# An eight-core decoder layer in fp32: norm factors applied after the matmul instead of before it, and the per-layer-embedding stage placed inside the next tile's first FFN

## The chip, the cores and the metric

The kernel runs on all eight cores of one Trainium2 chip, two dies of four cores. Each core works on one of the eight prompt sequences and on 16 of the 128 sampled tokens, with no exchange between cores. The time is device microseconds (us) of the slowest core. Each execution is called fast or slow: slow when one die runs over 1% longer than the other at a lower granted TensorE clock, or when the run is over 1.5% above the fastest of its kernel.

Different chips were used for different batches of runs, and the kernel before took between 1880 and 1950 us on them. So I compare ratios to the kernel before from the same batch, and, inside the traces, a lost time that leaves the chip's own slower clock out (explained below). In the views of the profile PE is TensorE and PEld its weight loads, DVE is VectorE, ACT ScalarE, POOL GpSimd. PSUM is the memory into which matmuls write, here in eight banks; reading a result out of it is called evacuation. A word is four bytes on each of the 128 partitions.

## The reference, cut to what matters

```python
D_MODEL, BATCH, SEQ, DEC_BATCH, PLE_DIM, D_FF = 1024, 8, 2048, 128, 256, 2816

def rms_norm(x, g):
    return x * rsqrt(mean(x * x, -1) + 1e-6) * g

def swiglu(x, w_gate, w_up, w_down):
    return (silu(x @ w_gate) * (x @ w_up)) @ w_down

def decoder_layer(x, p, s0, conv0, ng, ...):
    h = x + 0.5 * rms_norm(swiglu(rms_norm(x, ng[0]), f1_gate, f1_up, f1_down), ng[1])
    mix, s_new, conv_new = token_mixer(rms_norm(h, ng[2]), ...)   # linear attention in chunks + short conv
    h = h + rms_norm(mix, ng[3])
    h = h + 0.5 * rms_norm(swiglu(rms_norm(h, ng[4]), f2_gate, f2_up, f2_down), ng[5])
    gate = sigmoid(rms_norm(h, ng[6]) @ w_ple_gate)
    h = h + rms_norm((p @ w_ple_proj) * gate, ng[7])
    return h, s_new, conv_new
# ... called once for the prompt and once for the sampled tokens; all fp32
```

There are four stages (FFN1, mixer, FFN2, per-layer embedding), and each has a norm before it and a norm after it. The factor of a norm, rsqrt(mean(x*x)), is one number for a token. So (x*g) @ W times the factor is the same as the normalised x @ W: the factor may be applied after the matmul.

## The kernel before

A core cuts its 2048 tokens into eight tiles of 256 (the third has 272: the sampled tokens ride along). Two tiles, "slot 0" and "slot 1", go through the layer side by side and form a pair; they share every weight piece while it is in the chip. The features lie on the partitions, so the mean over features is a matmul with a matrix of 1/1024, and a factor for each token comes out on all partitions.

The order of the instructions of each engine is fixed when the program is built: generators yield operations, and a list scheduler with its own cost figures emits the one that can start first. On TensorE slot 0 goes first until it is LEAD words of weights ahead. Dependencies become semaphore waits.

```python
RING_W = 19456      # words per partition of the weight ring
LEAD = 8192         # slot 0's lead, in words of weights: 64 matmuls

# scheduler's own cost of a DMA:
self.dma_free = max(self.dma_free, start + 1.0) + op.nbytes / 320e3
self.fin[tok] = self.dma_free + 1.2

# pieces of weights in the order of their use; FFN columns are 2048 words (1 MB), then 1408 for the down projection
def w_issue():                                   # the ring: strictly first in, first out
    while wst["next"] < len(pieces):
        p = pieces[wst["next"]]
        lo = wst["head"]
        if lo + p["words"] > RING_W: lo = 0
        hi = lo + p["words"]
        live = wst["live"]
        while live and not live[0]["users"]: live.pop(0)     # a piece leaves when BOTH tiles have used it
        if any(q["at"] < hi and lo < q["at"] + q["words"] for q in live): return
        # ...
        P.emit_op(dma("pool", ...))

def h_squares(x): ...            # squares of h on ScalarE, sums on VectorE
def stats(x, scale=1.0):
    bk, = yield get_banks(1)
    yield mm(bk.v(0, x.n), [(csr.v(C_OD, C_OD + 128, r=True), x.accr())])      # mean by matmul
    yield act(x.lnt(), bk.v(0, x.n), AF.Ln, scale=scale, bias=eps)
    put_banks(bk)
    yield act(x.rs(), x.lnt(), AF.Exp, scale=-0.5)
def normalize(x, g):
    for c in range(8):
        yield stt(x.ch(x.xn, c, r=True), x.ch(x.h, c), ngl.v(g*8+c, ...), x.rs(), ALU.mult, ALU.mult)
def pre_norm(x, g):
    yield from h_squares(x); yield from stats(x); yield from normalize(x, g)
def post_norm(x):
    yield from stats(x)
    for q in range(4):                           # two 128-row chunks at a time
        yield tt(f2r, f2, rsb, ALU.mult)         # stage's result times its factor
        yield tt(h2, h2, f2, ALU.add)            # into the residual h

def slot(s):
    for t in range(s, NT, 2):
        x = T(t)
        yield lambda: True if t in loaded else None
        yield from pre_norm(x, 0)
        yield from ffn(x, 0, 1)                  # ends with post_norm
        yield from pre_norm(x, 2)
        yield from mixer(x)                      # ends with post_norm
        load_p(t)
        yield from pre_norm(x, 4)
        yield from ffn(x, 1, 5)
        yield from pre_norm(x, 6)
        yield from ple(x)
```

## Time and profile before

| | before |
|---|---|
| median of 3 runs (lowest to highest; the highest is a slow one) | 1880.64 us (1880.24 to 2009.39) |
| profiled fast run: span | 1891.0 us (core 4) |
| matmuls on each core | 11,554 |
| TensorE / VectorE / ScalarE busy | 79% / 42% / 36% |

The page of the profiled run begins with the span and the busy time of each engine (us, share, number of instructions):

```profile
span 1891.0 us, 33733 instructions; the slowest of 8 cores (1873.6 to 1891.0 us)
...
PE 1498.2 (79%) x11554; PEld 1464.5 (77%) x11554; DVE 787.8 (42%) x1730; ACT 684.0 (36%) x1533; POOL 222.6 (12%) x425
```

The list of what TensorE waited for (engine, written tile, source line <- who released it: total us, times, longest). L265 is the helper that emits nearly every matmul, L311 and L318 are VectorE helpers:

```profile
PE ps_pair L265 <- DVE sb_acc L311: 210.8, 33, 34.3
PE ps_pair L265 <- DVE sb_xn L318: 118.3, 23, 6.6
PE ps_pair L265 <- DVE sb_big L311: 23.4, 13, 5.3
```

The first line is the wait for the last addition of a sum of squares, the second the wait for normalised activations: 329 us together, of which 34.3 us is the start of the program and about 295 us are norms between stages. Nothing in this list is a DMA: the before never waits for weights.

One seam of this kind in the timeline of TensorE (start, length, operation, number of instructions, in brackets the idle time before it and what ended it): FFN2 to embedding stage to the next pair's FFN1.

```profile
1371.80 4.02 PE L265 MATMUL ps_pair<-sb_big,sb_ring 128*128 128x256 f32 x34
1377.80 0.35 PE L265 MATMUL ps_pair<-sb_acc,sb_csr 128*128 128x256 f32 x1 [1.99 <-DVE sb_acc L311]
1386.65 0.55 PE L265 MATMUL ps_pair<-sb_acc,sb_csr 128*128 128x256 f32 x1 [8.50 <-DVE sb_acc L311]
1391.79 2.05 PE L265 MATMUL ps_pair<-sb_xn,sb_ring 128*128 128x256 f32 x8 [4.58 <-DVE sb_xn L318]
```

The statistics matmul at 1377.80 belongs to the norm after FFN2, the one at 1386.65 to the norm before the embedding stage, and only at 1391.79 do the stage's own matmuls begin: 1.99 + 8.50 + 4.58 us of idle TensorE. Some 50 us later, before the next FFN1, it comes again.

**How I count lost time.** At full clock, matmuls with 256 columns start 118 ns apart. I took the start of every matmul from the trace. Where the next start comes more than 0.4 us later, the excess over 118 ns is a *pause*; where it comes sooner but the clock record says half speed, the excess is *half clock*. At a granted clock of 0.81 the spacing is 134 ns; I count that apart, because it depends on the chip. The matmuls are put to stages by the order of the program. All such numbers here are means over the eight cores. Before: 372 us pauses + 74 us half clock = 446 us lost (and 4 us at 0.81).

### The profile page before, as it was taken

The numbers are of one execution on the slowest core, as the hardware profiler recorded it, in microseconds if no ns is written. First come the engines' busy times: TensorE is split into PE (matmuls) and PEld (weight loads), VectorE is DVE, ScalarE is ACT, GpSimd is POOL, SyncE is SP. The second block draws the span as 40 slices with busy tenths as digits, with TensorE's granted clock in tenths as the row PEclk, the third lists the DMA queues.
The fourth block names the chain that finished last, engine by engine and source line by source line (L and its number), as shares of the span: only waits on it lengthen the run. The fifth ranks groups of instructions, "written<-read, shape, count | busy, mean of one in ns | idle before, by whom it ended". The sixth has DMA issues, their size and how long they took to land.

```text
span 1891.0 us, 33733 instructions; the slowest of 8 cores (1873.6 to 1891.0 us)
## 1 busy us (share of the span) xinstructions
PE 1499.8 (79%) x11554; PEld 1465.7 (78%) x11554; DVE 787.9 (42%) x1730; ACT 684.1 (36%) x1533; POOL 222.6 (12%) x425
## 2 busy tenths in 40 slices
PE   1797977996699686879658987869964996977964
PEld 1797877996599685779658987769964996967964
DVE  1223663115621576521454227642166216652145
ACT  1223464124522443422353234642244224552234
POOL 1011010110011110011100110101200120101100
PEclk9899897886799896789878998979977998988987
DMA  9499373984689662569855994739944995746951
GB/s 279 132 312 293 94 221 115 288 236 149 202 256 276 192 196 90 184 194 290 230 146 166 323 271 130 217 103 314 274 143 156 282 287 177 212 145 206 288 153 48
DMA packets 71334, 391.09 MB, mean 207 GB/s; under 512 B 8432, under 2 KB 9088, under 8 KB 38912
## 3 DMA queue, kind: packets, MB, share of 16 engines
q0 software_dynamic: 60512, 369.36, 65.3%
q1 hardware_dynamic: 10656, 19.58, 3.5%
q8 instruction: 97, 1.59, 0.3%
q14 instruction: 69, 0.57, 0.1%
HBM read 378.16 MB, written 10.75 MB: 206 GB/s over the span
## 4 chain that ended last, share of the span: by engine, by line
PE 71%; DVE 14%; issue 7%; ACT 5%; DMA 1%; DVEq 0%; SPq 0%; ACTq 0%
PE ps_pair L265 70%; DVE sb_xn L318 4%; ACT sb_scl L306 4%; DVE sb_h L311 2%; DVE sb_xn L311 2%; DVE sb_scl L311 2%; DMA sb_bg<-bg 1%; DVE sb_om L318 1%; PE ps_pair L276 1%; ACT L306 1%; DVE sb_big L311 1%; DVE sb_acc L311 1%; DVE sb_ring L311 0%; ACT sb_xn L306 0%; DVEq L218 0%
## 5 line engine op out<-in xcount | busy, mean ns | idle before, releaser
L265 PE MATMUL ps_pair<-sb_xn,sb_ring 128*128 128x256 f32 (+1 forms) x7424 | 974.2, 292 | 106.1 <-DVE sb_xn L318 98.4
L265 PEld LDWEIGHTS ps_pair<-sb_xn,sb_ring 128*128 128x128 f32 x7424 | 955.3, 201 | 114.0 <-issue 113.5
L311 DVE TENSOR_TENSOR sb_big<-ps_pair,sb_tmp 128x256 fp32r<-128x256 f32 (+1 forms) x384 | 163.3, 426 | 574.6 <-PE ps_pair L265 514.2
L306 ACT ACTIVATE sb_tmp<-ps_pair 128x256 f32<-128x256 f32 (+1 forms) x480 | 182.4, 384 | 532.8 <-PE ps_pair L265 528.0
L265 PE MATMUL ps_pair<-sb_big,sb_ring 128*128 128x256 f32 (+1 forms) x2816 | 347.0, 284 | 0.0
L265 PEld LDWEIGHTS ps_pair<-sb_big,sb_ring 128*128 128x128 f32 x2816 | 342.6, 192 | 0.0
L311 DVE TENSOR_TENSOR sb_scl<-sb_scl 128x256 f32<-128x256 f32 (+3 forms) x288 | 147.7, 515 | 326.2 <-ACT sb_scl L306 317.2
L265 PE MATMUL ps_pair<-sb_acc,sb_csr 128*128 128x256 f32 (+1 forms) x64 | 26.3, 411 | 209.5 <-DVE sb_acc L311 209.5
L265 PEld LDWEIGHTS ps_pair<-sb_acc,sb_csr 128*128 128x128 f32 x64 | 14.7, 230 | 216.9 <-issue 216.4
L306 ACT ACT_TABLE_LOAD x93 | 119.3, 1283 | 129.0 <-PE ps_pair L265 123.8
L306 ACT ACTIVATE sb_scl<-ps_pair 128x256 f32<-128x256 f32 (+1 forms) x192 | 73.9, 385 | 246.2 <-PE ps_pair L265 228.6
L318 DVE SCALAR_TENSOR_TENSOR sb_xn<-sb_h,sb_ngl,sb_scl 128x256 fp32r<-128x256 f32 (+1 forms) x256 | 104.7, 482 | 28.0 <-ACT sb_scl L306 27.5
L306 ACT ACTIVATE sb_scl<-sb_h 128x512 f32<-128x512 f32 (+1 forms) x128 | 76.4, 626 | 101.5 <-DVE sb_scl L311 96.2
L346 POOL DMA_DIRECT2D sb_ring<-f2a x88 | 46.5, 528 | 471.8 <-PE ps_pair L265 435.9
L346 POOL DMA_DIRECT2D sb_ring<-f1a x88 | 46.5, 533 | 467.5 <-PE ps_pair L265 467.5
L265 PE MATMUL ps_pair<-sb_om,sb_ring 128*128 128x256 f32 (+1 forms) x512 | 68.5, 295 | 6.6 <-DVE sb_om L311 6.6
L265 PEld LDWEIGHTS ps_pair<-sb_om,sb_ring 128*128 128x128 f32 x512 | 66.6, 201 | 8.1 <-issue 8.0
L311 DVE TENSOR_TENSOR sb_xn<-sb_xn,sb_scl 128x512 fp32r<-128x512 f32 (+1 forms) x96 | 66.3, 691 | 10.2 <-ACT sb_scl L306 9.0
L311 DVE TENSOR_TENSOR sb_h<-sb_h,sb_xn 128x512 f32<-128x512 f32 (+1 forms) x96 | 66.2, 692 | 4.5
L306 ACT ACTIVATE sb_xn<-ps_pair,sb_nglh 128x256 fp32r<-128x256 f32 (+1 forms) x128 | 60.3, 471 | 0.0
L306 ACT ACTIVATE sb_scl<-ps_pair,sb_cst 128x256 f32<-128x256 f32 (+2 forms) x80 | 41.2, 515 | 41.3 <-PE ps_pair L265 40.6
L346 POOL DMA_DIRECT2D sb_ring<-f2b x64 | 33.8, 530 | 145.9 <-PE ps_pair L265 145.7
(84 smaller groups left out, 824.9 us busy)
## 6 DMA issues: line engine op xcount, KB each, us to landing
sb_ring<-f1a POOLq DMA_DIRECT2D x88, 1024.0 KB, 11.7
sb_ring<-f2a POOLq DMA_DIRECT2D x88, 1024.0 KB, 10.3
sb_ring<-f1b POOLq DMA_DIRECT2D x64, 704.0 KB, 7.3
sb_ring<-f2b POOLq DMA_DIRECT2D x64, 704.0 KB, 7.1
sb_ring<-wca POOLq DMA_DIRECT2D x16, 1024.0 KB, 9.4
sb_ring<-wo POOLq DMA_DIRECT2D x16, 1024.0 KB, 10.9
sb_ring<-wpg POOLq DMA_DIRECT2D x16, 1024.0 KB, 7.3
sb_ring<-wv POOLq DMA_DIRECT2D x8, 1024.0 KB, 7.0
```

The lines of the kernel that those rows point to most:

```text
L265: ins = e.matmul(out.ap, a.ap, b.ap, start=(first and i == 0), stop=(last and i == n_ - 1), skip_group_check=skip)
L276: ins = e.matmul(o.ap, a.ap, b.ap, start=s, stop=t)
L306: return Op("act", lambda e: e.activation(out=out.ap, in_=in_.ap, func=func, **kw), rd, [out], 0.24 + 0.000833 * width(out), TSET.get(func))
L311: return Op(eng, lambda e: e.tensor_tensor(out=out.ap, in0=a.ap, in1=b.ap, op=op), [a, b], [out], 0.19 + width(out) / 960.0)
L318: return Op("dve", lambda e: e.scalar_tensor_tensor(out=out.ap, in0=a.ap, scalar=sc, in1=b.ap, op0=op0, op1=op1), rd, [out], 0.19 + width( ...
L346: return Op(eng, lambda e: e.dma_start(out=out, in_=in_), reads, writes, 0.55 if eng == "pool" else 0.1, None, name, nbytes, is_output)
```

## The change

The intent is to take the norms off TensorE's path in three ways.

1. *Deferral.* At a boundary the residual is only multiplied by its weight g, and the first matmuls of a stage take that raw product. The factor is made meanwhile and applied when the results are read out of PSUM (mixer gates, three FFN2 columns, embedding gate); for the other matmuls a `renorm` multiplies the raw copy beside the work.
2. *Move.* The embedding stage is spawned beside the next tile of its slot: its matmuls and weights are mixed into the first columns of the next pair's FFN1. That tile's own first norm (`prep`) is made ahead, during FFN2.
3. *Order.* Boundary operations go first on VectorE and ScalarE, Ln and Exp stay together, slot 0 leads by 80 matmuls instead of 64. A fourth residual buffer takes space, so the ring shrinks.

```diff
-RING_W = 19456
+RING_W = 16896
+NRAW = 3
+PLE_AT = (3, 5, 7, 9)
-LEAD = 8192
+LEAD = 10240
# ... cut: priorities (first, hold, free) of operations and their use in the scheduler
-        hb = [P.sbuf(f"h{i}", 128, 8 * TW) for i in range(3)]
+        hb = [P.sbuf(f"h{i}", 128, 8 * max(W_T[i::4])) for i in range(4)]
# ... weights of the embedding stage go between FFN1 columns of the next pair
+            def ple_w(pr, i):
+                piece((pr, "pg", i), wpg_d[...], 2048, tl)
+                piece((pr, "pp", i), wpp_d[...], 512, tl)
                 for j in range(NJ):
                     piece((pr, "a", f, j), fA_d[f][...], 2048, tl)
+                    if f == 0 and pr and j in PLE_AT:
+                        ple_w(pr - 1, PLE_AT.index(j))
# ... the boundary
-        def pre_norm(x, g):      # squares, statistics, eight multiplications
-        def post_norm(x):        # statistics, four times (multiply, add)
+        def boundary(x, g, buf):
+            yield from stats(x, [x.accr(0), x.accr(1)], x.rs(0))
+            x.pre = yield ("spawn", next_stats(x))            # next factor, beside the work
+            for q in range(4):
+                yield tt(x.pair3(f2r), x.pair3(f2), x.rs2(0), ALU.mult).first()
+                yield tt(x.ch(x.h, 2*q, 2), x.ch(x.h, 2*q, 2), f2, ALU.add).first()
+                hs.append((yield ("spawn", scaled(x, q, g, buf))))   # h * g, no factor, on ScalarE
+            yield join(hs)
# ... an FFN column on raw input: the factor at evacuation
+            if raw:
+                yield join([x.pre])
+                yield tt(t.v(0, x.n), bg_.v(0, x.n), x.rs(1), ALU.mult)
+                yield act(t.v(0, x.n), t.v(0, x.n), AF.Silu)
+                yield tt(t.v(0, x.n), t.v(0, x.n), x.rs(1), ALU.mult)
# ... FFN1 may overwrite the embedding stage's products from its column 14 on
+                if j == NJ - 8 and x.last:
+                    yield join([x.last])
# ... cut: sampled tile's values on GpSimd, merged additions of squares
         def slot(s):
+            tiles[s].prep = yield ("spawn", prep(tiles[s]))
             for t in range(s, NT, 2):
-                yield from pre_norm(x, 0)
                 yield from ffn(x, 0, 1)
-                yield from pre_norm(x, 2)
                 yield from mixer(x)
                 load_p(t)
-                yield from pre_norm(x, 4)
                 yield from ffn(x, 1, 5)
-                yield from pre_norm(x, 6)
-                yield from ple(x)
+                last = yield ("spawn", ple(x))
+                if t + 2 < NT:
+                    tiles[t + 2].last = last
```

## The prediction

> **What bounds the kernel now.** TensorE. The page shows it busy for 1500 of 1891 us, VectorE 42%, ScalarE 36%, DMA 207 GB/s. By the starts of core 0's matmuls, 10,765 of 11,554 run at full clock, 118 ns apart; 788 at half clock, 213 ns apart; 386 us are 95 pauses over 0.6 us. Without pauses and half clock the matmuls need about 1367 us. The list of waits names the pauses: TensorE waited 211 us in 33 waits for the last addition of a sum of squares and 118 us in 23 for the normalised activations; all others are below 25 us, none for weights. So 329 us are norms between stages; half clock costs about 74 us more (788 x 95 ns).
>
> One pair of tiles takes 447 us (1266 to 1713), of which 2872 matmuls need 339. Its pauses in the timeline: FFN1 to mixer 15 us, mixer and its end about 19, mixer to FFN2 14, FFN2 to embedding stage 16, embedding stage to next FFN1 20 + 6.
>
> **What the change does.**
> 1. The next matmul no longer waits for squares, sum, Ln, Exp and eight 0.48 us multiplications (14 us from the statistics matmul at 1377.8 to the first product at 1391.8). There remain last evacuation, one statistics matmul, Ln and Exp (0.9 us), four times two 0.69 us VectorE operations, one ScalarE scaling: 9 to 10 us. The lead of one tile over the other grows from 64 to 80 matmuls (9.4 us), which about fills that. Mixer gates and three FFN2 columns run on raw input while the second statistic is made.
> 2. The embedding stage moves inside the next FFN1; both its boundaries vanish for three of four pairs. The next tile's first norm is made ahead. About 42 us per pair.
> 3. Table loads (93 x 1.28 us; the Trainium skill, "ScalarE: Activation LUTs", What ACT_TABLE_LOAD costs, gives the same 1283 ns) leave the chain: Ln's table is fetched early, Ln and Exp stay together.
> 4. The sampled tile's state update uses GpSimd and half the matmuls, beside the chunk work. That pair took 494 us, 47 over the others; about 25 back.
>
> Added: VectorE multiplications for raw evacuations (0.4 us each, few). The ring shrinks from 19,456 to 16,896 words while the lead takes 10,240: prefetch falls from 5.5 to 3.3 pieces (12 us of work); median landing is 11.4 us. FFN needs about 280 GB/s at full clock and dense slices reach 330, so I expect few DMA waits.
>
> **Sum (estimate).** 1367 + 40 start + 36 end + 4 x 22 remaining pauses + 25 half clock = 1556; plus about 50 for contention in the static order, DMA waits and clock: 1605 us.
>
> **Clock.** The Trainium skill ("TensorE: Matmul & The Clock Gate", Part 1) says three dense cores take a die to 13/16. Here dense FFN stretches of all eight cores mostly ran at 1.00; only cores 4 and 5 were at 0.81, for 140 us. Denser work may meet it oftener: all at 0.81 (134 ns a matmul) gives about 1780.
>
> **Chances.** Faster by over 2%: 0.95; within 2%: 0.03; slower: 0.02. Eight in ten: 1530 to 1715.
>
> **What would show it.** FFN2 to next FFN1 without a pause over 3 us; waits on squares and normalised activations under 90 us; TensorE busy over 88%; half-clock matmuls under 350; TensorE's DMA waits under 30 us.
>
> **What would make it wrong.** TensorE waiting for weights (shorter prefetch); evacuations delayed by ScalarE held for Ln and Exp, so PSUM runs out; the embedding stage unfinished before FFN1's last eight columns; the 0.81 clock becoming the rule; boundaries staying at 10 us because both tiles' VectorE work collides.

## The result, and the profile after

The changed kernel took a median of 1765.8 us in four runs (1759.61 to 1788.76, one of them slow), against 1887.2 us of four runs of the kernel before (one of them slow too). Ratios here are the mean time of one kernel's fast runs over that of the other's of the same rounds, so not quite the ratio of the medians. This one is 0.936 (95% interval 0.928 to 0.943). Faster was right, but 1766 us lies outside the predicted range, 1530 to 1715: of the expected 276 us (1880.64 less 1605), 115 came. Two later repeats on other chips gave 0.928 and 0.9325.

The page after, the answer to the lines shown above:

```profile
span 1760.3 us, 33650 instructions; the slowest of 8 cores (1745.3 to 1760.3 us)
...
PE 1492.7 (85%) x11642; PEld 1462.7 (83%) x11642; DVE 768.4 (44%) x1668; ACT 789.0 (45%) x1801; POOL 242.1 (14%) x441
```

TensorE does the same work in a shorter span (88 more matmuls: statistics in several terms). The two dies are alike in this run: a median of 1756.0 and 1754.5 us for their cores, at granted clocks of 0.930 and 0.929.

The list of what TensorE waited for. L291 and L302 are the matmul helpers of this kernel:

```profile
PE ps_pair L291 <- DVE sb_smr L337: 43.3, 2, 36.7
PE ps_pair L291 <- DVE sb_acc L337: 39.9, 9, 8.2
PE ps_pair L302 <- DVE sb_big L337: 27.8, 7, 9.6
PE ps_pair L291 <- DMA sb_ring<-f1a: 23.2, 17, 5.8
PE ps_pair L291 <- DMA sb_ring<-f2a: 16.6, 12, 3.9
PE ps_pair L291 <- POOL sb_ring L337: 12.2, 5, 4.3
PE ps_pair L291 <- DMA sb_ring<-wpp: 11.1, 5, 3.3
```

The 210.8 us before statistics matmuls have shrunk to 114 us: 43.3 + 39.9 above, 9.0 for a square on ScalarE, and 22 that the list credits to the writer of another tile (the view of the lines, by form, gives 62.2 + 8.5 + 43.3 us of idle time before these matmuls; not shown). Of this, 36.7 is the one wait at the start of the program. The 118 us for normalised activations have shrunk to 10.3, at the start of the two slots, besides 6.9 us before the first FFN2 matmuls of pairs 3 and 4 that the list credits to another tile (not shown). In their place stand waits that were not there before: weights by DMA, f1a (FFN1 columns), f2a (FFN2 columns), wpp (embedding).

The seam that took 15 us before each embedding stage is closed. TensorE's timeline from FFN2's down projection into the next FFN1:

```profile
1260.65 17.20 PE L291 MATMUL ps_pair<-sb_big,sb_ring 128*128 128x256 f32 x143
1277.68 0.40 PE L291 MATMUL ps_pair<-sb_acc,sb_csr 128*128 128x256 f32 x2
1277.92 2.06 PE L291 MATMUL ps_pair<-sb_xn,sb_ring 128*128 128x256 f32 x16
```

No idle time stands in brackets. (At the other two seams of this kind the longest wait at the seam is 0.2 us; some 31 us after each of the three seams, inside FFN1, the statistics of tile 1's next norm wait 3.1, 3.3 and 2.6 us.) But inside the following FFN1 there are pauses that the before did not have (same view, later; the lines left out have no idle time):

```profile
1364.31 1.11 PE L291 MATMUL ps_pair<-sb_om,sb_ring 128*128 128x256 f32 x8
1369.29 2.88 PE L291 MATMUL ps_pair<-sb_xn,sb_ring 128*128 128x256 f32 x16 [3.87 <-DMA sb_ring<-f1a]
...
1381.28 2.13 PE L291 MATMUL ps_pair<-sb_xn,sb_ring 128*128 128x256 f32 x16 [1.23 <-DMA sb_ring<-f1a]
1386.00 14.20 PE L291 MATMUL ps_pair<-sb_xn,sb_ring 128*128 128x256 f32 x105 [2.59 <-DMA sb_ring<-f1a]
```

Lost time by stage (pauses + half clock, us, sum over the four pairs), before and after:

| stage | before | after | after, pairs 1 to 4 |
|---|---|---|---|
| FFN1 columns (after: with embedding inside, pairs 2 to 4) | 41 | 75 | 17, 20, 19, 19 |
| FFN1 down projection, to the mixer | 67 | 13 | |
| mixer, to FFN2 | 107 | 121 | 18, 51, 27, 26 |
| FFN2 columns | 66 | 55 | 19, 7, 14, 14 |
| FFN2 down projection, to the next stage | 63 | 3 | |
| embedding stage alone | 102 | 31 | last pair only |
| **sum** | **446** | **296** | |

Pairs are counted from 1 here; the expectations count them from 0. Pair 2 holds the sampled tile. The seams are gone (67 to 13, 63 to 3); the FFN columns together got no better (107 to 130), and the mixer neither.

### The profile page after: what moved, and what is told of

Same layout as the page of the kernel before. It is cut to its first block, busy times and chain, and to the rows that moved or that the text cites. A ratio compares the mean times of both kernels' runs of the same rounds, so it can differ in the third digit from the quotient of the medians.

```text
span 1760.3 us, 33650 instructions; the slowest of 8 cores (1745.3 to 1760.3 us)
## 1 busy us (share of the span) xinstructions
PE 1492.7 (85%) x11642; PEld 1462.7 (83%) x11642; DVE 768.4 (44%) x1668; ACT 789.0 (45%) x1801; POOL 242.1 (14%) x441
## 4 chain that ended last, share of the span: by engine, by line
PE 65%; DMA 12%; DVE 9%; ACT 7%; issue 5%; DVEq 0%; POOL 0%; SPq 0%; ACTq 0%; POOLq 0%
PE ps_pair L291 64%; DMA sb_ring<-f1a 8%; DVE sb_h L337 2%; DMA sb_ring<-f2a 2%; DVE sb_xn L337 2%; ACT L332 2%; ACT sb_scl L332 1%; DMA sb_bg<-bg 1%; DVE sb_om L337 1%; PE ps_pair L302 1%; ACT ps_pair L332 1%; DVE sb_scl L337 1%; ACT sb_xn L332 1%; DMA sb_ring<-wpp 1%; DMA sb_ring<-f1b 1%
## 5 line engine op out<-in xcount | busy, mean ns | idle before, releaser
L291 PE MATMUL ps_pair<-sb_xn,sb_ring 128*128 128x256 f32 (+1 forms) x3968 | 530.5, 293 | 39.3 <-DMA sb_ring<-f1a 13.6
L291 PE MATMUL ps_pair<-sb_om,sb_ring 128*128 128x256 f32 (+1 forms) x3968 | 521.9, 291 | 36.4 <-DVE sb_om L344 10.3
L291 PEld LDWEIGHTS ps_pair<-sb_xn,sb_ring 128*128 128x128 f32 x3968 | 513.4, 199 | 45.7 <-issue 45.5
L291 PEld LDWEIGHTS ps_pair<-sb_om,sb_ring 128*128 128x128 f32 x3968 | 507.8, 198 | 42.3 <-issue 42.1
L291 PE MATMUL ps_pair<-sb_big,sb_ring 128*128 128x256 f32 (+1 forms) x2816 | 348.8, 282 | 1.1 <-DMA sb_ring<-f1b 0.8
L291 PEld LDWEIGHTS ps_pair<-sb_big,sb_ring 128*128 128x128 f32 x2816 | 342.3, 188 | 1.9 <-issue 1.6
L332 ACT ACTIVATE sb_tmp<-ps_pair 128x256 f32<-128x256 f32 (+1 forms) x360 | 136.0, 384 | 376.8 <-PE ps_pair L291 375.9
L337 DVE TENSOR_TENSOR sb_scl<-sb_scl 128x256 f32<-128x256 f32 (+3 forms) x208 | 101.7, 491 | 219.9 <-ACT sb_scl L332 218.1
L332 ACT ACTIVATE sb_scl<-ps_pair 128x256 f32<-128x256 f32 (+2 forms) x240 | 95.6, 399 | 197.7 <-PE ps_pair L291 178.8
L332 ACT ACT_TABLE_LOAD x109 | 139.8, 1283 | 74.0 <-PE ps_pair L291 59.2
L291 PE MATMUL ps_pair<-sb_acc,sb_csr 128*128 128x256 f32 (+1 forms) x136 | 32.3, 342 | 70.7 <-DVE sb_acc L337 39.9
L291 PEld LDWEIGHTS ps_pair<-sb_acc,sb_csr 128*128 128x128 f32 x136 | 24.2, 229 | 75.3 <-issue 75.1
L332 ACT ACTIVATE sb_tmp<-sb_tmp 128x256 f32<-128x256 f32 (+1 forms) x88 | 36.0, 418 | 98.0 <-DVE sb_tmp L337 97.7
L337 DVE TENSOR_TENSOR sb_tmp<-ps_pair,sb_scl 128x256 f32<-128x256 f32 (+1 forms) x88 | 36.9, 423 | 49.9 <-PE ps_pair L291 49.8
L332 ACT ACTIVATE sb_scl<-sb_h 128x512 f32<-128x512 f32 (+1 forms) x72 | 45.2, 630 | 27.3 <-DVE sb_h L337 12.0
L337 DVE TENSOR_TENSOR sb_xn<-sb_xn,sb_scl 128x512 fp32r<-128x512 f32 (+1 forms) x56 | 40.6, 726 | 24.8 <-ACT sb_scl L332 22.2
L332 ACT ACTIVATE ps_pair<-ps_pair,sb_cst 128x256 f32<-128x256 f32 (+3 forms) x82 | 39.9, 487 | 25.2 <-PE ps_pair L291 24.4
## 6 DMA issues: line engine op xcount, KB each, us to landing
sb_ring<-wg POOLq DMA_DIRECT2D x8, 1024.0 KB, 12.2
```

Source lines behind the costliest of these rows:

```text
L291: ins = e.matmul(out.ap, a.ap, b.ap, start=(first and i == 0), stop=(last and i == n_ - 1), skip_group_check=skip)
L332: return Op("act", lambda e: e.activation(out=out.ap, in_=in_.ap, func=func, **kw), rd, [out], 0.19 + 0.000833 * width(out) + (0.09 if isi ...
L337: return Op(eng, lambda e: e.tensor_tensor(out=out.ap, in0=a.ap, in1=b.ap, op=op), [a, b], [out], 0.16 + width(out) * (2.6 / 1200 if eng = ...
```

## The experiments

Theories at the outset. **Ring**: the smaller ring with its first-in-first-out order, and the embedding weights in it, makes TensorE wait for weights. Its rivals: **contention** of both tiles' boundary work on VectorE; **half clock and the 0.81 clock**; the **move** itself being worth less than booked. The kernels ran in five batches; a batch shares one chip and its runs of the kernel before. "Loss" is pauses plus half clock.

| run | ratio to before | median us | loss | FFN1 col. | FFN2 col. | mixer | embedding | DMA waits |
|---|---|---|---|---|---|---|---|---|
| after (first run) | 0.936 | 1765.8 | 296 | 75 | 55 | 121 | 31 | 52 |
| c1, unedited | 0.928 | 1813.3 | 285 | 70 | 53 | 119 | 31 | 40 |
| c2, unedited | 0.9325 | 1763.1 | 292 | 73 | 54 | 119 | 31 | 50 |
| e1 half the bytes | 0.900 | 1737.9 | 259 | 51 | 45 | 119 | 31 | 24 |
| e2 weights later | 0.931 | 1801.4 | 282 | 72 | 54 | 117 | 31 | 46 |
| e3 stage outside | 0.933 | 1801.4 | 285 | 20 | 53 | 112 | 97 | 24 |
| e4 no raw start | 0.939 | 1816.0 | 294 | 71 | 50 | 123 | 31 | 31 |
| e5 half the pieces | 0.853 | 1663.6 | 169 | 15 | 19 | 100 | 31 | 1 |
| e6 chunk first | 0.929 | 1812.0 | 289 | 69 | 49 | 127 | 31 | 43 |
| e7 weights twice | 0.931 | 1815.1 | 290 | 78 | 67 | 108 | 31 | 47 |
| e8 first fit | none | 1808.8 | 294 | 71 | 73 | 107 | 31 | 55 |
| e9 smaller ring | none | 1852.8 | 349 | 101 | 59 | 124 | 31 | 86 |
| b1 before, small ring | none | 1945.4 | 451 | 43 | 72 | 107 | 100 | 2 |
| e10 first fit, 2.8 us | none | 1777.5 | 250 | 41 | 56 | 105 | 31 | 8 |
| e11 e10, stage outside | 0.929 | 1755.9 | 291 | 20 | 55 | 105 | 101 | 11 |
| e12 2.8 us only | 0.926 | 1750.2 | 277 | 67 | 38 | 126 | 31 | 34 |
| e13 first fit, 1.3 us | 0.921 | 1765.8 | 266 | 52 | 69 | 104 | 30 | 32 |
| e14 values on VectorE | 0.933 | 1777.3 | 294 | 70 | 54 | 124 | 31 | 50 |
| e15 e10 again | 0.918 | 1747.4 | 251 | 43 | 56 | 105 | 31 | 9 |

The before ran at 1929.5 us with e1 to e4, 1950.3 with c1 and e5 to e7, 1946.3 with e8 to e10 and b1, 1891.1 with c2 and e11 to e13, and 1903.8 with e14 and e15. In the third batch many executions were slow, so no ratio was given; the profiles of e8, e10 and b1 fell in the slow state, and of those I use the losses, which leave the 0.81 clock out, and no ratio. "DMA waits" is the sum of TensorE's waits for weights by DMA on the profiled core.

The three runs of the unedited kernel lose 285 to 296 us, so differences of less than about 10 us of loss say nothing here. Its ratio differs from chip to chip too, 0.928 to 0.936, so ratios of different batches are compared only beyond that. One warning for the columns: in e7, e8, e10, e11 and e13 part of pair 2's loss moves from the mixer (50 to 51 us in the unedited runs, 33 to 46 there) into FFN2 columns (7 us, and 20 to 30 there); for these runs the two columns are best read as a sum.

### Is it the weights? e1: half the bytes, same order

Wrong results: after the first 60, each piece transfers only its first half; the scheduler is told the old size, so the order is the same.

```diff
-  P.emit_op(dma("pool", ..., dst.ap, p["src"], [], [dst], 128 * 4 * p["words"]))
+  cut = p["words"] // 2 if wst["next"] > 60 else p["words"]
+  P.emit_op(dma("pool", ..., p["buf"].v(0, cut, r=True).ap, p["src"][:, 0:cut], [], [dst], 128 * 4 * p["words"]))
```

> Changed kernel with every weight transfer after the first 60 cut to half its columns (wrong result on purpose); ring, program order and all waits stay the same, because the kernel's own planner still counts full bytes. Theory S, weights come late because the ring's space is freed late and in bursts: landing gets about half as long, so the pauses of the FFN1 columns with the embedding stage inside (15 to 18 us a pair on core 0) and the waits on f1a, f2a and wpp (51 us in the list of waits) fall to under a third: 1700 to 1735 us. Theory E, the columns pause because evacuations or the order hold TensorE up: no change, 1750 or more.

Loss fell by about 26 us (FFN1 columns 70 to 51), so weights matter, but most of the lost time stayed. Its time fell by more than that, because it lost only 17 us at the 0.81 clock against 48 to 51 in the other three of this batch; half the bytes also means other data in the matmuls, and which of the two lowered that, I did not test.

### e2: the embedding weights later in the order

```diff
-PLE_AT = (3, 5, 7, 9)
+PLE_AT = (7, 9, 11, 13)
```

> Changed kernel with the embedding weights loaded after FFN1 columns 7, 9, 11, 13 instead of 3, 5, 7, 9. Theory S in its sharper form, the embedding weights sit at the head of the first-in first-out ring and are released only when the second tile's embedding stage has used them, so the FFN weights behind them are asked for late: FFN1 columns lose 12 us a pair instead of 24, total 1720 to 1740 us. If the hold is not the cause (or the wait for the finished embedding stage before column 14 takes over): within 10 us of the changed kernel.

No gain (loss 282). The result was **wrong** (relative error 0.07). From the code: column 13 of the 272-wide tile occupies words 3536 to 3808 of its buffer, and the embedding products of the tile before begin at word 14 x 256 = 3584, while the guard waits only ahead of column 14. The changed kernel is right in all its runs, by this reading only because its embedding stage ends sooner in its order; from e8 on, wherever I edited the order, the guard is one column earlier for that tile. This cause is read from the code; no run isolates it. The instructions and their waits are as planned, so I still read its time, but only as a hint.

### e3: the embedding stage outside, everything else kept

```diff
-                    if f == 0 and pr and j in PLE_AT:
+                    if False:
# ... embedding weights after FFN2 of the same pair, and
-                last = yield ("spawn", ple(x))
-                if t + 2 < NT:
-                    tiles[t + 2].last = last
+                yield from ple(x)
```

> Changed kernel with the embedding stage put back between FFN2 and the next FFN1, weights behind FFN2's; deferred norms, early first norm and everything else kept. My prediction said the move is worth 42 us a pair, 126 us in all: that would give about 1885 us less what the faster norms save. If ring waits in FFN1 give most of it back, this run is between 1765 and 1800 us. Below 1755 would mean that the move costs time.

This undoes the move alone, and costs nothing: ratio 0.933, loss 285. The stage by itself then loses 97 us (21, 22, 22, 31), against 31 inside; but FFN1 columns lose 20 instead of 70 to 75. The move takes 22 us out of each of three pairs and puts about 18 back as waits in FFN1 columns, and some 10 us in all go to the FFN1 down projection (11 to 13 us in the unedited runs, 2 here). So as written the move is worth nothing, and the whole gain comes from deferral, the norm made ahead and the order.

### e4: no raw start

```diff
-NRAW = 3
+NRAW = 0
# mixer: the gates' matmuls moved behind the renorm
-            yield from g_proj(x, m)
             yield join([x.ren])
+            yield from g_proj(x, m)
```

> Changed kernel that waits for the second statistic and the multiplied activations before the mixer gates and before FFN2, so no matmul of these stages starts on raw input (NRAW 0; gates still multiply at evacuation). If the raw start hides the second statistic as intended, 8 boundaries a run for each of two tiles lose 2 to 6 us each where the other tile does not fill it: 1775 to 1810 us. If the other tile's lead covers it anyway: within 10 us of the changed kernel.

The ratio is 0.939 against 0.931 to 0.933 of e2 and e3 in the same batch, some 0.7%; the loss of 294 lies within the 285 to 296 of the unedited kernel. Feeding matmuls with raw input is at most a small part of the gain. How the rest divides between the shorter boundary, the norm made ahead, the order and the longer lead no run shows.

### c1: the changed kernel again

No edit of the changed kernel; the control of its batch.

> The changed kernel itself, unedited, as the control of this call. Same chip behaviour as the first measurement would give 0.936 of the kernel before; the chip of the last call held TensorE at 0.81 for long stretches, in which case about 0.93 to 0.94 and pauses plus half-clock loss as before, about 296 us.

Ratio 0.928 on a chip where 69 us went to the 0.81 clock (first run: 0). The kernel before lost time there too (1950 us), so the ratio hardly moved. That clock is not why the prediction failed.

### e5: pieces of half the size, so twice the room and half the bytes

Wrong results: every piece has half its words in the ring, the matmuls read the half that is there (same number, same shapes), LEAD keeps its meaning, and the order is planned anew.

```diff
-  pieces.append({..., "words": words, ...})
+  pieces.append({..., "words": {2048: 1024, 1408: 768, 1024: 512, 512: 256}[words], ...})   # but not the sampled state
# reads of a piece wrap into its half
+class Half(Buf):
+    def v(self, lo, hi, ...):
+        w = hi - lo
+        o = lo % self.W if lo % self.W + w <= self.W else 0
+        return Buf.v(self, o, o + w, p0, p1, r)
```

> Changed kernel with every weight piece halved, in the ring and in its transfer (matmuls read the same half twice; wrong result on purpose), so the ring holds about 16 FFN columns instead of 8; the planner makes its order anew. The run with half the bytes alone still lost 259 us in pauses and half clock, 52 of them in FFN1 columns and 45 in FFN2 columns. Theory S, ring space held by the other tile: FFN1 columns of pairs 1 to 3 fall below 5 us each, FFN2 columns below 8 each, total loss near 190 us, time about 0.89 of before. Rival, bytes alone: as the half-byte run, 0.90 and 259 us. In both the mixer keeps its 115 to 125 us.

The loss fell to 169 us, FFN1 columns from 70 to 15, FFN2 columns from 53 to 19. The list of TensorE's waits begins like this; all DMA waits together are 0.8 us:

```profile
PE ps_pair L291 <- DVE sb_smr L337: 29.6, 1, 29.6
PE ps_pair L302 <- DVE sb_big L337: 25.5, 5, 8.2
...
PE ps_pair L291 <- DMA sb_ring<-f1a: 0.8, 1, 0.8
```

Of the 116 us under its control (285), e1 had shown 26 to come from the bytes. Of the other 90, about 17 are FFN1 columns of pair 1 (17 in e1, none here): e1 left these transfers whole, so they may be bytes too. The other 73 or so come with the room, or with the order that was planned for it and for the shorter transfers. This is the largest single effect. The mixer still loses 100: that part is something else.

### e6: whose turn on VectorE

In the mixer of pair 3 TensorE stood still for 9.62 us. Four lines of the timeline of the changed kernel, all engines:

```profile
1125.98 0.40 PE L302 MATMUL ps_pair<-sb_big 128*128 128x256 f32 x2
...
1128.58 0.69 DVE L337 TENSOR_TENSOR sb_om<-sb_om,sb_scl 128x512 fp32r<-128x512 f32 x1
...
1135.17 0.68 DVE L337 TENSOR_TENSOR sb_big<-ps_pair,sb_cst 128x512 fp32r<-128x512 f32 x1
...
1136.00 0.55 PE L302 MATMUL ps_pair<-sb_big,sb_Sr 128*128 128x256 f32 x1 [9.62 <-DVE sb_big L337]
```

From 1128.58 VectorE works off tile 0's eight boundary operations, which go first. Tile 1's chunk waits for one multiplication with the mask, its scores made by 1126.4, and gets it at 1135.17; 0.8 us later TensorE goes on. If this collision costs the mixer its time, letting the chunk's short operations go ahead should give it back.

```diff
+    def urgent(self):
+        self.pri = -1
+        return self
-   viewed(cst.v(C_MK, C_MK + 128), ...), ALU.mult)
+   viewed(cst.v(C_MK, C_MK + 128), ...), ALU.mult).urgent()
# likewise the chunk's square, state updates and copy of the state
```

> Changed kernel in which the GLA chunk's mask multiplication, square and state update go ahead of the boundary operations that the change put first. In the changed kernel TensorE stood 9.8 us (pair 2) and about 7 us (pair 3) for a mask multiplication that waited behind eight boundary operations of the other tile on VectorE. Theory Q, this queueing is what keeps the mixer as long as before: mixer pauses fall by 4 to 9 us in pairs 0, 2, 3; 15 to 25 us in all. Rival: the wait only moves to the other tile's first FFN2 matmul, which then starts later: change below 8 us in all.

No gain: ratio 0.929, mixer 127. The pause did not vanish, it changed its name: the list of waits has no long wait for that multiplication any more, but

```profile
PE ps_pair L295 <- ACT sb_om L336: 22.3, 5, 9.7
...
PE ps_pair L295 <- DVE sb_tmp L348: 9.7, 1, 9.7
```

each with a longest wait of 9.7 us. With both tiles in need of VectorE at the same moment, somebody's work is late. So contention in the mixer is real, and a different priority does not remove it.

### e7: embedding weights loaded once for each tile

Pieces are held until the slower tile has used them. In the trace of the changed kernel, pair 4 on core 0 (from the order of the program and the DMA starts): FFN1 columns 13 and 14 were requested at 1361.9, 0.8 us after tile 1's last matmul on the third embedding piece had started (1361.1); column 13 was first used at 1369.3. Columns 16 to 20 were requested at 1374.7 to 1376.9, after tile 1's last matmul on the fourth (started at 1373.9), and column 16 was used at 1381.3. GpSimd, which issues the weights, shows it as long rests and bursts:

```profile
1343.55 1.58 POOL L372 DMA_DIRECT2D sb_ring<-f1a  x3 [0.18 <-issue]
1361.94 1.08 POOL L372 DMA_DIRECT2D sb_ring<-f1a  x2 [16.80 <-PE ps_pair L291]
...
1374.69 2.71 POOL L372 DMA_DIRECT2D sb_ring<-f1a  x5 [10.67 <-PE ps_pair L291]
```

And the DMA view of 1343 to 1390 us, 40 slices of 1.2 us (first line busy share in tenths, second GB/s):

```profile
DMA  2699999990000505006999999980669999999999
GB/s 9 101 288 418 439 411 425 418 377 21 0 0 0 223 0 199 24 14 98 314 370 361 417 404 413 418 321 16 70 258 418 342 272 251 265 321 284 282 335 312
```

The engines move over 400 GB/s for some slices, then next to nothing in seven of the nine slices from 1353.6 to 1364.2, while column 13 waits for room. Bandwidth was not short, requests were: the mean that I had compared with 330 GB/s hid it. If holding for tile 1 is the whole cause, a copy for each tile should end it:

```diff
-PLE_AT = (3, 5, 7, 9)
+PLE_AT = ((3, 5, 7, 9), (7, 9, 11, 13))
-            def ple_w(pr, i):                     # users: both tiles
+            def ple_w(pr, i, s):                  # users: tile s alone
```

> Changed kernel that loads the embedding weights once for each tile (5.2 MB more a pair), the first tile's after columns 3, 5, 7, 9, the second's after 7, 9, 11, 13, so that no piece waits in the ring for the slower tile's embedding stage. Correct result expected. Theory S: the bursts of freed space go, FFN1 column loss of pairs 1 to 3 falls from 19 to under 10 us each; time 15 to 30 us under the control. If bytes or the number of pieces decide instead: as the control or slower.

It did not: loss 290, FFN1 columns 78. The copies need room and transfers of their own, which may be why; no run separates that. So the holding is seen in the trace, but this remedy against it is worth nothing.

### e8, e12, e10: two ways to request earlier, alone and together

e8 replaces first in, first out by the gap that has been free longest. e12 keeps that order and only tells the scheduler that a transfer takes 2.8 us longer; the kernel is otherwise the same, but its fixed order asks less of weights that have just been requested. e10 does both. The reason for e12: the scheduler believes in 1.0 + 3.28 + 1.2 = 5.5 us for 1 MB, while in the changed kernel's trace (core 0) 1 MB pieces on which TensorE waited were first used 5.1 to 8.4 us after their request where no other had been requested just before, and 9.8 to 24.8 us where they stood behind others.

```diff
# e8, e10: where to put the next piece
+  live = wst["live"] = [q for q in wst["live"] if q["users"]]
+  edges = sorted((q["at"], q["at"] + q["words"]) for q in live) + [(RING_W, RING_W)]
+  # ... gaps that are wide enough, at either end
+  lo = min(gaps, key=lambda g: (ring_time(g, g + p["words"]), g))
# e12, e10: what the scheduler believes
-  self.dma_free = max(self.dma_free, start + 1.0) + op.nbytes / 320e3
-  self.fin[tok] = self.dma_free + 1.2
+  self.dma_free = max(self.dma_free, start + 2.0) + op.nbytes / 320e3
+  self.fin[tok] = self.dma_free + 3.0
# all three: the guard of e2's fault, one column earlier for the 272-wide tile
-  if j == NJ - 8 and x.last:
+  if j == NJ - 8 - x.samp and x.last:
```

> Changed kernel whose ring is no longer first-in first-out: a new piece takes any free place long enough, the one that was left longest ago, so a piece held for the slower tile's embedding stage blocks only its own place. One wait is added: FFN1 of the wider tile waits for the embedding stage one column earlier (column 13 of a 272-wide tile overlaps the first product of a 256-wide one; that is what made the late-embedding run wrong). Theory S, head-of-line blocking in the ring: FFN1 columns of pairs 1 to 3 lose 8 to 12 us each instead of 19, total loss 285 to about 255, time 0.91 to 0.92 of before (control 0.928). If space itself, not its order, is short: total loss stays above 275 and the ratio within 0.005 of the control. FFN2 columns stay near 53 in both.

> Changed kernel with its first-in first-out ring, planner's landing 2.8 us longer and nothing else. If the fixed order's optimism about landing is the whole cause: as the first-fit run with that figure, 0.910 to 0.918 and about 250 us lost. If the ring must also be freed out of order to use it: 0.925 or more, because the planner then only knows that it waits.

> As the first-fit run, with the kernel's own planner told that a weight transfer takes 2.8 us longer (in the traces a piece that is asked for late is used 6 to 7 us after its issue; the planner's figure is about 5.4). Only the program order changes. If TensorE stands because its fixed order comes to a column before the weights have landed, 5 to 15 us less than the first-fit run; if the planner's figure was near enough, the same or slower by up to 10 us.

First fit alone: loss 294, no gain, so the strict order alone is not the cause. Longer belief alone: 277, ratio 0.926 against 0.9325 of c2 in the same batch; FFN2 columns fell from 54 to 38. Both: 250, FFN1 columns 41, DMA waits 8. The two gain more together than their sum. My reading, not shown by a run of its own: an earlier request needs a free gap, and a free gap helps only if the order does not count on the piece too soon.

### e9 and b1: less room

```diff
# e9, on the changed kernel       # b1, on the kernel before
-RING_W = 16896                   -RING_W = 19456
+RING_W = 14848                   +RING_W = 16896
```

> Changed kernel with one FFN column (2048 words) less ring: 14,848. Theory S says ring space is the price: doubling it in effect took about 90 us more than halving the bytes, so one piece of eight less costs 15 to 35 us, in FFN1 and FFN2 columns. If space is not the limit: within 8 us of the control, ratio 0.928 to 0.932.

> The kernel before with the changed kernel's ring, 16,896 words instead of 19,456. If the old order, in which the tiles stop together at every norm, has ring space to spare: 1.000 to 1.008 of before. If space costs the old kernel as much as the new: 1.015 or more. Its profile also shows the clock and the pauses of the old order on this chip.

One FFN column less (2048 words) costs the changed kernel 58 us over its mean loss (291), more than the 15 to 35 expected: 349. DMA waits rise to 86 us, the largest of them:

```profile
PE ps_pair L291 <- DMA sb_ring<-wpp: 29.4, 9, 5.8
...
PE ps_pair L291 <- DMA sb_ring<-f1a: 26.7, 11, 6.0
```

The kernel before does not mind the changed kernel's ring at all: loss 451 against 446, and medians of 1945 against 1946 us, both of slow executions only. So it is not the smaller ring as such. I read it so: TensorE of the kernel before stands still at each seam, and the DMA can catch up there; with the seams closed, a longer lead and the embedding weights in between, the same ring is too small. Which of these three matters most is not shown; no run changes the lead alone. But room had become a limit, and the profile of the kernel before does not show it as a wait.

### c2: the third look at the changed kernel

No edit.

> The changed kernel unedited, control of this call: 0.925 to 0.937 of before, 280 to 296 us of pauses and half clock.

Ratio 0.9325, loss 292, almost none at 0.81: the first result stands.

### e11: e10 with the embedding stage outside

The edits of e3 and e10 together (the guard is then not needed):

```diff
# e10's ring and scheduler figures, and from e3
-                last = yield ("spawn", ple(x))
+                yield from ple(x)
```

> Embedding stage outside FFN1, ring by first fit, planner's landing 2.8 us longer. If the move pays once the order allows for the landing: slower than the two inside runs of that kind, 0.93 to 0.94 of before (FFN1 free of pauses, embedding stage 20 us a pair), so the move is then worth 30 us or so. If the move gives nothing even then: 0.91 to 0.92.

Loss 291, ratio 0.929, against 250 and 251 with the stage inside (e10, e15; ratio 0.918). With weights requested in time, the move does pay: 40 us of loss, about 13 for each of the three pairs. (e11 and e15 ran on different chips, so the losses, which e10 and e15 repeat within 1 us, carry this more than the ratios do.) Outside, first fit and longer belief bring nothing (291 against e3's 285).

### e13: first fit with a smaller correction

e10 with a smaller correction, 1.3 us in all:

```diff
-  self.dma_free = max(self.dma_free, start + 2.0) + op.nbytes / 320e3
-  self.fin[tok] = self.dma_free + 3.0
+  self.dma_free = max(self.dma_free, start + 1.5) + op.nbytes / 320e3
+  self.fin[tok] = self.dma_free + 2.0
```

> Inside, first fit, planner's landing 1.3 us longer, near the 6.5 to 7 us of the traces. Between first fit alone (294 us lost) and the 2.8 us figure (250 us lost): 0.912 to 0.922. As good as the larger figure if matching the trace is what counts.

Loss 266, between e8 and e10; ratio of its fast runs 0.921 (0.920 to 0.9225). Three of its six executions were slow, so its median, 1765.8 us, is not a fast one; the fast ones took 1738 to 1745.

### e14: the sampled tile's values on VectorE

The change had moved a product of the sampled tile to GpSimd, and TensorE waits 12.2 us for it (shown above).

```diff
-                                 ALU.mult, "pool")
+                                 ALU.mult)
```

> Changed kernel with the sampled tile's masked value products on VectorE instead of GpSimd, everything else kept. If GpSimd is what holds the sampled mixer: its loss falls from 50 us by 8 to 12 us, ratio 0.927 or less. If VectorE, which also carries both boundaries there, is as tight: unchanged or up to 15 us slower.

No gain: ratio 0.933, mixer of pair 2 54.7 us against 50 to 51 in the three unedited runs. GpSimd is not what keeps that pair long.

### e15: e10 on a chip with fast runs

The same kernel as e10, no edit.

> First fit and a landing 2.8 us longer in the planner, embedding stage inside; the earlier run lost 250 us and took 1777.5 us where the kernel before took 1946 (many executions in the slow state). The outside run of the same kind had 0.9288 and lost 291 us. If the move pays 35 to 40 us once the order fits: 0.905 to 0.915 of before, and faster than both kernels.

Ratio 0.918 (0.916 to 0.920), loss 251, the same as e10. The page of its profile:

```profile
span 1745.2 us, 33583 instructions; the slowest of 8 cores (1720.6 to 1745.2 us)
...
PE 1515.8 (87%) x11642; PEld 1490.2 (85%) x11642; DVE 765.2 (44%) x1668; ACT 782.5 (45%) x1797; POOL 240.7 (14%) x441
```

Its median, 1747.4 us, stands beside 1777.3 us of e14 (a changed kernel in all but one product) on the same chip: 1.7% less. With e11, e12 and e13 it is correct, and the fast runs of all four lie below those of both kernels on their chip: below the changed kernel by 0.4% (e11) to 1.7% (e15, for which e14 stands for the changed kernel).

## Why the prediction was wrong

The predicted sum and what core 0's trace of the changed kernel shows for each term:

| term | predicted | measured | difference |
|---|---|---|---|
| matmuls at 118 ns | 1367 | 1374 (11,642 of them) | +7 |
| start | 40 | 37 | -3 |
| end | 36 | 14, and some 26 of pauses in the last embedding stage | +4 |
| other pauses | 88 (4 x 22) | 213 (239 less those 26) | +125 |
| half clock | 25 | 66 (671 matmuls) | +41 |
| delays under 0.4 us | none | 31 (before: 11) | +31 |
| sum before contingency | 1556 | 1761 (span 1760.3) | +205 |

The contingency of 50 us covered a quarter of it.

**The step that failed** is this one: "prefetch falls from 5.5 to 3.3 pieces ... dense slices reach 330, so I expect few DMA waits". I compared rates, and the limit was room and time of request. A piece frees its room when the *slower* tile has used it; the transfer can be asked for only then; and it takes 5 to 8 us to be usable, more behind other pieces. I had the warning numbers (the ring, the lead, the landing time) and let a mean rate overrule them. TensorE's DMA waits were 51.7 us, not under 30, and they are only the visible part: e5 shows 116 us that go with the pieces' size, some 73 of them with room and order rather than bytes. The list of waits credits a pause to the last release only, which is why 52 us of listed waits can stand for more. The chain of work that ended last (the profile's critical view) shows it directly. Its shares of the span, before and after, in lines that the view cuts off:

```profile
by line: PE ps_pair L265 69.5%; issue 7.3%; DVE sb_xn L318 4.2%; ACT sb_scl L306 3.6%; DVE sb_xn L311 2.3%; DVE sb_h L311 2.2%; DVE sb_scl L311 1.7%; DMA sb_bg<-bg 1.3%; DVE sb_om L318 1.2%; ACT L306 1.1%; PE ps_pair L276 1.1%; DVE sb_big L
...
by line: PE ps_pair L291 64.0%; DMA sb_ring<-f1a 7.8%; issue 5.2%; DVE sb_h L337 2.3%; DMA sb_ring<-f2a 1.8%; DVE sb_xn L337 1.8%; ACT L332 1.8%; ACT sb_scl L332 1.5%; DMA sb_bg<-bg 1.4%; DVE sb_om L337 1.3%; PE ps_pair L302 1.2%; ACT ps_pa
```

Transfers into the ring are no part of the chain before; after, all of them together are 189 us of it (150 in c2). In e9 they are 248, in e15 63, in e5 8. (TensorE works during most of this time, so it is not time lost; it tells what the next matmuls hung on.) The Trainium skill ("Perfetto Trace Analysis", Optimization Strategy) says that consistent bubbles on the engine that should be saturated can mean too little SBUF (the on-chip memory in which the ring lies) for the next tile; e5 and e9 agree, with 15 and 101 us lost in FFN1 columns against 70 to 75.

**A second term failed too**: "4 x 22 remaining pauses". The mixer alone lost 121 us where it had lost 107 before: its boundaries stayed, with waits on VectorE such as the 9.6 us of e6. Of the 205 us by which the sum was short, e10 gives back 41 and e5, with half the bytes, at most 116 or so; the rest, much of it in the mixer, is not explained by these runs. (The ratio of e5, 0.853, would make about 1610 us of 1887, near the predicted 1605. That may be luck in part, since its mixer still loses 100 us.)

**Point by point.**

- *Norms off the path* (point 1): right for the seams after the FFNs, with longer waits than said. FFN1's and FFN2's down projections with their seams went from 67 and 63 us to 13 and 3. At the seam from FFN2 to the next FFN1 there is no pause over 3 us, as said. But waits on squares and normalised activations came to about 124 us (114 and 10.3), not under the 90 named.
- *"About 42 us per pair" for the move* (point 2): wrong. The seams hold 16 (FFN2 to embedding) and 26 (the stage). e3, without the move, already lost only 0.4 a pair in the first; 22 of the 26 remained. So the move itself could give 22, and gave back about 18 in FFN1 columns, by ring waits among others, and 3 to 4 in the FFN1 down projection. Its worth as written is nil (e3), and 40 us in all once weights come in time (e11 against e15).
- *Table loads leave the chain* (point 3): they did not. In the chains above, the table loads (ACT L306 and L332, which name no tile) have 1.8% of the span, 31 us, against 1.1%, 21 us, before. There were 109 loads instead of 93, of 1283 ns each in both traces, the figure of the Trainium skill ("ScalarE: Activation LUTs", What ACT_TABLE_LOAD costs):

```profile
L332 ACT ACT_TABLE_LOAD x109 | 139.8, 1283 | 74.0 <-PE ps_pair L291 59.2
```

- *Sampled tile, "about 25 back"* (point 4): wrong. The mixer of its pair lost 53.5 us before and 51 after. GpSimd was cleared by e14; what does hold it stays open (in e7, e8, e10, e11 and e13 part of it moved to FFN2 columns).
- *Boundaries colliding on VectorE* had been named as a risk, and did come: the 9.6 us pause of pair 3 is one. e6 shows that priority only moves the wait. FFN1 down and mixer together still fell from 174 to 134 us. The mixer's own 100 us, which even e5 keeps, is not settled by these runs.
- *Half clock, 25 us*: wrong in size, 66 us (671 matmuls, not under 350). I had taken shorter pauses for harmless. The Trainium skill ("TensorE: Matmul & The Clock Gate", Part 1) gives half clock after at least one idle window of about 3.4 us. Here less was enough, by the clock records and by matmuls 213 ns apart: on core 0 of the kernel before, one gap of 2.1 us between matmul starts (from 1385.3) was followed by half clock from 1387.4 to 1394.2; of the changed kernel, a gap of 2.8 us (from 1305.7) by half clock from 1308.9 to 1312.4. So pauses split into several of 2 to 3 us can keep the half clock.
- *The 0.81 clock* as the reason: no. The profiled run after lost 0 us to it, and c1, which lost 69, has nearly the same ratio to the kernel before on its chip (0.928 against 0.936).
- *TensorE over 88% busy*: it was 85%.

What stays open: how the gain of e5 divides between bytes, more room and the order planned for it; whether the longer lead, which no run undoes, takes the room that is missing; why the mixer keeps 100 us; and why e1 lost less at the 0.81 clock.

## What to carry to other kernels

When pauses are taken out of an engine, ask what used to be refilled in those pauses: a prefetch buffer that never shows as a wait can become the next limit, and it should be judged by when its room comes free (the slower of its users) plus the time to land, not by mean bandwidth. Test each part of a compound change by undoing it alone; here the part booked at 42 us a pair was worth nothing until the requests were mended. And when the order of instructions is fixed at build time from cost figures, check the figure for a transfer against the trace: 2.8 us more, together with a less strict ring, was worth 1 to 2% over the changed kernel.

## What the Trainium skill lacked or had wrong

- "TensorE: Matmul & The Clock Gate", Part 1: the clock is said to fall to half after at least one idle window of about 3.4 us. In these traces one gap of 2.1 us inside otherwise dense work was followed by 6.8 us at half clock, and 2.8 us by 3.4 us.
- The same page and part: three dense cores are said to take a die to 13/16 within 5 to 20 us. On two chips all eight cores ran dense FFN stretches at full clock, 118 ns a matmul, and lost only 0 to 5 us at 0.81 in a whole run (mean of the cores; the changed kernel 0 and 1.7); on another the changed kernel lost 69 us. It differed from chip to chip here.
- "DMA: Bandwidth & Descriptors", Bandwidth, Measured: 6.15 us and 341 GB/s for 1 MB is the busy time of the transfer alone. In a kernel, a 1 MB piece on which TensorE waited, requested with no other just before it, was first used 5.1 to 8.4 us after its issue, which agrees roughly; of twelve pieces requested in bursts (1343 to 1390 us) the median landed after 10.3 us, while slices of 1.2 us reached 411 to 439 GB/s. The page gives no such figure for a queue of pieces.
- None of the pages that I read speaks of a weight ring that two tiles share, where the slower one frees the room: 116 us of 285 us lost went with the size of its pieces.
